# Opening stage of a two-block kernel: order of the loads, four more buffers for the modulation weights, and the memory norm summed on TensorE

## Chip, core and metric

The kernel runs on one core of a Trainium2 chip. A core has engines that each run their own list of instructions in order: TensorE (PE, with its weight loads as PEld), VectorE (DVE), ScalarE (ACT), GpSimd (POOL) and SyncE (SP). Data moves between HBM and on-chip memory by DMA; a DMA is issued by one of these engines, and in this kernel before the change by SP nearly always. The metric is the device time of one execution in microseconds (us), lower is better.

## The reference

The computation is two transformer blocks on 512 tokens of width 1024, in float32. The first block has two layers with a stream of 512 tokens and a context of 256 tokens; the second has latent attention, a long convolution (hyena), attention to 256 memory tokens, and a mixture of experts. The change touches what is needed at the start of the first block, and two things of the second block that depend on no activation and are made at the start:

```python
# first block, for l = 0 and 1
mx = jnp.split(silu_c @ w_mod[l] + b_mod[l], 6, axis=-1)      # "modulation", for the stream
mc = jnp.split(silu_cc @ w_mod[l] + b_mod[l], 6, axis=-1)     # and for the context
ax = modulate(rmsnorm(h, norm1_g[l]), mx[0], mx[1])
ac = modulate(rmsnorm(hc, norm1_g[l]), mc[0], mc[1])
yx, yc = mixing_layer(ax @ w_in[l], ac @ w_in[l], ...)         # pool mixing, neighborhood attention, retention
# second block
kf = _hyena_filters(S, hy_w1, hy_b1, hy_freq, hy_w2, hy_b2, hy_w3, hy_b3, hy_decay)
k, v = jnp.split(_rms(mem, mem_norm_g) @ w_mkv, 2, axis=-1)   # keys and values of the memory
```

`_hyena_filters` is two sine layers of width 64, a third layer times an exponential decay, and a Fourier transform over 512 positions (a product with a matrix here).

## The kernel before

Activations lie with channels on the partitions, 8 tiles of 128 channels by 512 tokens (256 for the context and the memory). A product with a weight keeps float32 accuracy by three matmuls on parts (L198 to L200): the weight is loaded (L180, 512 KB a piece, tile `wraw`, 4 buffers), rounded by ACT (L181, `whi`) and its remainder made by DVE (L182, `wlo`); the activation has a rounded part (L268 or L348, names ending in h) and a remainder (L269 or L349, names ending in l).

`first()` (L1671) makes the opening from generators, each of which does one step when it is asked: `memory()` (letter m), `modulation(0, 0)` (d), `hyena_filters()` (f), the loads of the stream (h) and the norm of the stream (n). The strings `START` and `SECOND` say whose turn it is. A tile scheduler then puts the instructions of all engines in an order, in which each engine runs its own, without overtaking. SP's list of DMA issues is one such order: an issue whose buffer is not free yet, or whose data are not there yet, holds up all issues behind it. Each of SP's DMAs also waits until the eighth before it has landed.

- `modulation(l, r)` makes a third of the six modulation vectors of a layer: 16 loads of 512 KB (L409, tile `mraw`, 2 buffers), each read by a pair of float32 matmuls with 2 columns of output partitions (L412, tile `bg`); at the end ACT copies the sums (L417, `mrow`), four small matmuls turn them (L420) and DVE adds the bias (L424). r = 0 holds what the first norm needs; r = 1 and 2 are taken a step at a time beside the neighborhood attention and the retention of layer 0 (`beside` and `tick`).
- `memory()` loads the 256 memory tokens (L1446), norms them, and makes keys (8 pieces of `w_mk`, written to HBM by L1456) and values (8 pieces of `w_mv`, written by L1472). Its norm is the common one: ACT squares a tile (L327), POOL adds it to a sum (L328, `sqacc`), PE sums over the partitions into a column (L301), ACT takes the square root (L289), DVE the reciprocal (L290), PE spreads it over the partitions again (L314), ACT copies it (L317, `rstd`), DVE multiplies (L340).
- `hyena_filters()` makes the two sine layers (L1147, and L1115 to L1125 for the sine; ACT's last step gives `hh`), the third layer (L1173, with L1175 the exponential and L1176 the product) and the transform, and writes it to HBM (`kf`, L1201; `kx`, L1210).
- After the opening, layer 0 begins: the norm of stream and context with the modulation (`ah`, `al`), the pool mixing (`pool_steps`: products with `w_in` into the `lin` and `sc` banks, which ACT copies to `px`, L825; POOL adds windows, L842 to L853), then for each pair of heads the neighborhood attention (`na_unit`: scores L240, softmax L498) and the retention (`ret_pair`). The bias of the neighborhood attention is loaded and masked by POOL (L580, L583) once the pool mixing's memory is free.

Of the kernel before, what the change touches and what calls it, by code (L numbers as in the profile page):

```python
# [11 lines left out]
F32 = mybir.dt.float32  # L12
# [3 lines left out]
ALU = mybir.AluOpType  # L16
AX = mybir.AxisListType

P = 128
# [33 lines left out]
START = "m f m m m f f f m m f m f m m h h h h h h d f h f d d d d h f d d f d f d d m m m f d m n f f f d d n m m d d n m m d d n m n".split()  # L53
# [52 lines left out]
class Builder:  # L106
    def __init__(self, ctx, tc, a, out):
        self.tc, self.nc, self.a, self.out = tc, tc.nc, a, out
        pool = lambda name, bufs=1, **kw: ctx.enter_context(tc.tile_pool(name=name, bufs=bufs, **kw))
        self.cp = pool("const")  # L110
        self.sm = None
        self.ps = pool("psum", 8, space=bass.MemoryType.PSUM)
        self.uid = 0
        self.background = iter(())
        self.opened, self.seconds = {}, {}
        self.np, self.nw, self.ahead = None, S, 2
        self.turn, self.probs, self.pinned = True, 2, False
        self.meanwhile = iter(())
# [283 lines left out]
    def modulation(self, l, r):  # L402
# [3 lines left out]
        for k in range(KC):  # L406
            for half in range(2):
                raw = self.t([P, 1024], F32, "mraw", 2, self.modp)
                nc.sync.dma_start(raw, self.a["w_mod"][l, r, k, half])  # L409
                for g in range(2):  # L410
                    q = 32 * (2 * half + g)
                    nc.tensor.matmul(ps[q:q + 2, :], self.csil[:, k, :], raw[:, g * 512:g * 512 + 512],  # L412
                                     start=k == 0, stop=k == KC - 1, tile_position=(0, q))
                yield
# [712 lines left out]
    def hyena_filters(self):  # L1127
# [32 lines left out]
        for n in range(2):  # L1160
# [49 lines left out]
            nc.sync.dma_start(self.kx[n].rearrange("o r s -> (o r) s"), o[:3, 0])  # L1210
# [230 lines left out]
    def memory(self):  # L1441
# [7 lines left out]
        self.norm(m, (0, C), lambda k: self.col("mem_norm_g_2", k), None, mh, ml)  # L1449
        yield  # L1450
        self.mk = self.tc.dram_tile([KC, P, C], F32, name="mk_dram")
        for j in range(KC):
            ps = self.linear(self.weight(a["w_mk"][j], 1024), mh, ml, (0, C))
            x = self.t([P, C], F32, "mo", 2)
            nc.scalar.copy(x, ps)
            nc.sync.dma_start(self.mk[j], x)  # L1456
            yield
# [10 lines left out]
        for j in range(2):  # L1468
# [3 lines left out]
            nc.sync.dma_start(self.mv[j], x)  # L1472
# [198 lines left out]
    def first(self):  # L1671
# [16 lines left out]

        memory = within(memory_pool, self.memory())
# [6 lines left out]
        self.close("memory")  # L1696
# [666 lines left out]
```

## Time and profile before

| | us |
|---|---|
| median of 3 runs | 2606.75 (2606.6 to 2607.93) |
| the profiled execution | 2606.64 |
| its span | 2604.8 |
| PE busy, whole span | 2461.1 (94%) |
| DVE, ACT, POOL busy | 1707.2, 1169.6, 434.0 |
| PE busy in the first 200 us | 171.17 |
| PE busy from 200 to 600 us | 383.93 of 400 |

Times in the trace count from the start of the span. The list of waits of an engine names the line that waited, what released it, the sum, the number and the longest. A timeline row has the start, the busy time, the engine and line, the operation with output and input tiles, a count, and in brackets the idle time before it with its releaser. A float32 matmul shows as two records, so that a pair of modulation matmuls is "x4". [...]

### The profile page before, as it was taken

What the parts mean: (1) busy time and instruction counts of PE and PEld (TensorE: products, weight loads), DVE (VectorE), ACT (ScalarE), POOL (GpSimd) and SP (SyncE); (2) the same over time, 40 slices, a digit from 0 to 9 for tenths busy, and PEclk for the clock granted to TensorE, in tenths of its full rate; (3) what the DMA queues carried; (4) which work ended last, traced back from release to release, by engine and by line L of the source; (5) the groups of instructions that cost most, each with busy time, mean ns of one, the idle gap of its engine ahead of it and who ended that gap; (6) DMA issues with size and microseconds to landing.
All of it is one profiled execution on the core that took longest, in us unless ns stands there. A gap on an engine that the chain in (4) does not pass through costs nothing. (4 is left out here: it accounts for less than half of the span.)

```text
span 2604.8 us, 37537 instructions
## 1 busy us (share of the span) xinstructions
PE 2461.1 (94%) x14286; PEld 2002.3 (77%) x14286; DVE 1707.2 (66%) x2916; ACT 1169.6 (45%) x1971; POOL 434.0 (17%) x448
## 2 busy tenths in 40 slices
PE   6999999999999999998999999999999879989996
PEld 5568766788888888887877888888878777866664
DVE  6656776657667666566777664545788987535555
ACT  6555456655322313355555553424665655421112
POOL 3042121120000000043232200000600352031100
PEclk9999999999999999999999999999999999989998
DMA  7742222252335353252111533332421453379992
GB/s 236 267 151 87 86 90 98 65 171 86 96 119 160 99 174 108 66 174 77 50 43 55 165 97 97 94 100 91 128 71 51 162 192 122 112 269 405 415 417 120
DMA packets 114047, 368.90 MB, mean 142 GB/s; under 512 B 17988, under 2 KB 29648, under 8 KB 101450
## 3 DMA queue, kind: packets, MB, share of 16 engines
q1 hardware_dynamic: 110554, 358.10, 40.8%
q0 software_dynamic: 3312, 8.40, 0.9%
q8 instruction: 113, 1.85, 0.3%
q14 instruction: 68, 0.56, 0.1%
HBM read 356.95 MB, written 13.68 MB: 142 GB/s over the span
## 5 line engine op out<-in xcount | busy, mean ns | idle before, releaser
L198 PE MATMUL lin<-ah,whi 128*128 128x512 f32 (+1 forms) x1504 | 556.3, 370 | 19.9 <-ACT qd L224 9.3
L200 PE MATMUL lin<-al,whi 128*128 128x512 f32 (+1 forms) x1504 | 547.6, 365 | 1.5 <-DVE al L349 1.1
L199 PE MATMUL lin<-ah,wlo 128*128 128x512 f32 (+1 forms) x1504 | 545.5, 363 | 2.8 <-DVE wlo L182 2.8
L181 ACT CAST whi<-wraw 128x1024 fp32r<-128x1024 f32 (+2 forms) x297 | 297.5, 1004 | 309.6 <-PE sc L200 171.0
L182 DVE TENSOR_TENSOR wlo<-wraw,whi 128x1024 fp32r<-128x1024 f32 (+2 forms) x297 | 360.7, 1216 | 83.3 <-ACT whi L181 82.1
L198 PEld LDWEIGHTS lin<-ah,whi 128*128 128x128 f32 x1504 | 286.7, 191 | 69.8 <-ACT qd L224 11.2
L200 PEld LDWEIGHTS lin<-al,whi 128*128 128x128 f32 x1504 | 285.8, 190 | 50.0 <-issue 2.7
L199 PEld LDWEIGHTS lin<-ah,wlo 128*128 128x128 f32 x1504 | 286.6, 191 | 40.6 <-DVE wlo L182 3.3
L328 POOL TENSOR_TENSOR sqacc<-sqacc,sq 128x256 f32<-128x256 f32 (+1 forms) x101 | 129.7, 1289 | 1083.6 <-ACT sq L327 1082.3
L199 PE MATMUL sc<-ah,wlo 128*128 128x256 f32 (+1 forms) x696 | 219.7, 316 | 0.0
L198 PE MATMUL sc<-ah,whi 128*128 128x256 f32 (+1 forms) x696 | 219.6, 316 | 0.0
L200 PE MATMUL sc<-al,whi 128*128 128x256 f32 (+1 forms) x696 | 219.0, 316 | 0.0
L198 PEld LDWEIGHTS sc<-ah,whi 128*128 128x128 f32 x696 | 132.8, 191 | 10.7 <-issue 0.9
L199 PEld LDWEIGHTS sc<-ah,wlo 128*128 128x128 f32 x696 | 133.0, 191 | 10.0 <-DVE wlo L182 0.4
L200 PEld LDWEIGHTS sc<-al,whi 128*128 128x128 f32 x696 | 132.7, 191 | 8.1
L892 DVE SCALAR_TENSOR_TENSOR fv<-lin,vec,fv 128x511 f32<-128x511 f32 x67 | 50.1, 749 | 117.1 <-ACT fv L891 117.1
L450 DVE CUSTOM_DVE_ANT_0 mraw<-mraw,crow 128x512 f32<-128x512 f32 x128 | 86.8, 689 | 42.5 <-DMA mraw<-in_w_mod_rows 41.3
L199 PE MATMUL lin<-mh,wlo 128*128 128x512 f32 (+1 forms) x292 | 105.3, 361 | 1.5 <-DVE wlo L182 1.4
L198 PE MATMUL lin<-mh,whi 128*128 128x512 f32 (+1 forms) x292 | 105.3, 361 | 0.0
L200 PE MATMUL lin<-ml,whi 128*128 128x512 f32 (+1 forms) x292 | 104.8, 359 | 0.0
L1924 PE MATMUL lin<-ew,ex 128*64 128x256 f32 x864 | 98.7, 381 | 0.3 <-issue 0.3
L891 ACT ACTIVATE fv<-lin,vec 128x512 f32<-128x512 f32 x67 | 52.1, 778 | 102.1 <-PE lin L200 85.6
(642 smaller groups left out, 5297.8 us busy)
## 6 DMA issues: line engine op xcount, KB each, us to landing
ew<-in_w_moe SPq DMA_DIRECT2D x81, 1024.0 KB, 16.6
wraw<-in_w_up SPq DMA_DIRECT2D x88, 512.0 KB, 3.5
wraw<-in_w_in SPq DMA_DIRECT2D x61, 512.0 KB, 3.7
mraw<-in_w_mod SPq DMA_DIRECT2D x48, 512.0 KB, 3.5
mraw<-in_w_mod_rows SPq DMA_DIRECT2D x96, 256.0 KB, 2.8
wraw<-in_w_down SPq DMA_DIRECT2D x48, 448.0 KB, 3.3
wraw<-in_w_out SPq DMA_DIRECT2D x32, 512.0 KB, 3.6
wraw<-in_w_down SPq DMA_DIRECT2D x16, 512.0 KB, 3.5
```

The source lines that it names most:

```text
L181: nc.scalar.copy(hi[:, :n], raw[:, :n])
L182: nc.vector.tensor_tensor(out=lo[:, :n], in0=raw[:, :n], in1=hi[:, :n], op=ALU.subtract)
L198: mm(out, wh, xh, start=start, stop=False)
L199: mm(out, wl, xh, start=False, stop=False)
L200: mm(out, wh, xl, start=False, stop=stop)
L328: nc.gpsimd.tensor_tensor(out=acc, in0=acc, in1=sq, op=ALU.add)
L450: self.tc.keep_in_program_order(nc.vector.tensor_tensor_reduce(out=x, in0=raw, in1=self.crow[:, i, d], scale=1.0, scalar=0.0, op0=ALU.mult ...
L891: nc.scalar.activation(out=v[:, t0:t1], in_=ps, func=AF.Identity, scale=cw(1), bias=self.col("conv_b", 44 * l + f))
L892: nc.vector.scalar_tensor_tensor(out=v[:, t0 + 1:t1], in0=ps[:, :t1 - t0 - 1], scalar=cw(0), in1=v[:, t0 + 1:t1], op0=ALU.mult, op1=ALU.add)
L1924: self.pin(nc.tensor.matmul(ps[CAP * f:CAP * f + CAP, :256], xk, pieces(512 * k + 256 * f, 256), start=k == 0, stop=k == KC - 1, tile_posi ...
```

## The change

The string `START` is replaced: the filters' first step comes first, and from then on the memory's and the modulation's steps take turns from the beginning. The loads of `modulation(0, 0)` take their tiles from a pool of their own with 4 buffers (`modq`), open until `START` is used up; the later ones use the old pool with 2. For r = 1 and 2 of each layer the first matmul of each pair is kept in program order by the scheduler. The memory's norm squares its 8 tiles on ACT and DVE in turn, and 8 float32 matmuls with a 128x128 matrix of ones sum them over the partitions, so that each partition has the sum; the root and the reciprocal are taken of the 128x256 tile. The writes of `kx`, of the memory's keys and of its values are issued by ACT.

```diff
-START = "m f m m m f f f m m f m f m m h h h h h h d f h f d d d d h f d d f d f d d m m m f d m n f f f d d n m m d d n m m d d n m n".split()
+START = "m f m d m d f m d f m d f m d f m d m d f d m d f m d h f m d h f m d h f m d h f d h m f d h d h m d h n f n m n m n m n f".split()
...
         for k in range(KC):
             for half in range(2):
-                raw = self.t([P, 1024], F32, "mraw", 2, self.modp)
-                nc.sync.dma_start(raw, self.a["w_mod"][l, r, k, half])
+                pool, engine = (self.modp, nc.sync) if self.modq is None else self.modq
+                raw = self.t([P, 1024], F32, "mraw", 2 if self.modq is None else 4, pool)
+                engine.dma_start(raw, self.a["w_mod"][l, r, k, half])
                 for g in range(2):
                     q = 32 * (2 * half + g)
-                    nc.tensor.matmul(ps[q:q + 2, :], self.csil[:, k, :], raw[:, g * 512:g * 512 + 512],
-                                     start=k == 0, stop=k == KC - 1, tile_position=(0, q))
+                    ins = nc.tensor.matmul(ps[q:q + 2, :], self.csil[:, k, :], raw[:, g * 512:g * 512 + 512],
+                                           start=k == 0, stop=k == KC - 1, tile_position=(0, q))
+                    if r > 0 and g == 0:
+
+                        self.tc.keep_in_program_order(ins)
...
-            nc.sync.dma_start(self.kx[n].rearrange("o r s -> (o r) s"), o[:3, 0])
+            nc.scalar.dma_start(self.kx[n].rearrange("o r s -> (o r) s"), o[:3, 0])
...
-        self.norm(m, (0, C), lambda k: self.col("mem_norm_g_2", k), None, mh, ml)
+
+        ps = self.psum("pt")[:, :C]
+        for k in range(KC):
+            sq = self.t([P, C], F32, "mo", 2)
+            if k % 2:
+                nc.vector.tensor_tensor(out=sq, in0=m[k], in1=m[k], op=ALU.mult)
+            else:
+                nc.scalar.activation(out=sq, in_=m[k], func=AF.Square)
+            nc.tensor.matmul(ps, self.ones, sq, start=k == 0, stop=k == KC - 1)
+        r = self.t([P, C], F32, "mr", 1)
+        nc.scalar.activation(out=r, in_=ps, func=AF.Sqrt, scale=1.0 / D, bias=self.eps)
+        nc.vector.reciprocal(out=r, in_=r)
+        for k in range(KC):
+            nc.vector.tensor_tensor(out=m[k], in0=m[k], in1=r, op=ALU.mult)
+            self.affine_split(mh[k], ml[k], m[k], self.col("mem_norm_g_2", k))
         yield
...
-            nc.sync.dma_start(self.mk[j], x)
+            nc.scalar.dma_start(self.mk[j], x)
...
-            nc.sync.dma_start(self.mv[j], x)
+            nc.scalar.dma_start(self.mv[j], x)
...
+        self.modq = self.open("modq", "right"), nc.sync
...
-        self.close("memory")
+        self.close("modq", "memory")
+        self.modq = None
```

Line numbers of the changed kernel are up to 22 higher than those of before: its L181 is L180 of before, L411 is L409, L414 is L412, L1152 is L1147, L1178 is L1173, L1475 is L1456, L1733 is L1711, L302 and L315 are L301 and L314, L830 is L825. L1459, L1461 and L1462 are the new squares and their products.

SP's list of DMA issues, between the first loads of `w_mk` and the first load of the modulation; before:

```order
L1711 DMA hy_87<-in_hT 128x768
L1711 DMA hy_88<-in_hT 128x768
L1456 DMA mk_dram<-mo_251 128x256
L180 DMA wraw_536<-in_w_mk 128x1024
L1456 DMA mk_dram<-mo_285 128x256
L180 DMA wraw_570<-in_w_mk 128x1024
L1456 DMA mk_dram<-mo_319 128x256
L1711 DMA hy_89<-in_hT 128x768
L1711 DMA hy_90<-in_hT 128x768
L1711 DMA hy_91<-in_hT 128x768
L1456 DMA mk_dram<-mo_429 128x256
L409 DMA mraw_611<-in_w_mod 128x1024
```

and after, from the first load of `w_mk` on:

```order
L181 DMA wraw_222<-in_w_mk 128x1024
L411 DMA mraw_257<-in_w_mod 128x1024
L181 DMA wraw_261<-in_w_mk 128x1024
L411 DMA mraw_295<-in_w_mod 128x1024
L1162 DMA hskip_300<-in_hy_skip 1x1024
L1168 DMA hw_304<-in_hy_w3b 65x1024
L1170 DMA hdec_306<-in_hy_decay 128x1024
L181 DMA wraw_344<-in_w_mk 128x1024
L411 DMA mraw_378<-in_w_mod 128x1024
L181 DMA wraw_400<-in_w_mk 128x1024
L411 DMA mraw_434<-in_w_mod 128x1024
L181 DMA wraw_456<-in_w_mk 128x1024
```

Before, a write of keys (`mk_dram`) stands ahead of nearly every further load, and the first `mraw` comes behind four of these writes; after, loads of `w_mk` and `mraw` take turns, with no write among them.

ACT's list where the modulation r = 0 is done and the norm of the stream begins; before, from the last copy of `mrow` on:

```order
L417 COPY mrow_72<-bg_610 2x512 x4
L193 CAST wlo_1180<-wraw_1179 128x1024
L289 ACT_TABLE_LOAD
L289 ACTIVATE tokw_1077<-pt_1072,eps 128x4
L1471 COPY mvo_1068<-sc_764 128x512
L1471 COPY mvo_1068<-sc_765 128x512
L1198 COPY hodd_1130<-lin_1116 128x512
L317 COPY rstd_1085<-pt_1080 128x512
L181 CAST whi_1262<-wraw_1261 128x1024
```

and after, from the last casts of filter n = 0 on (the copies of `mrow` stand some thirty rows further up):

```order
L269 CAST hs1h_849<-hx_912 128x512
L1180 ACTIVATE he_965<-hdec_837,htc_121 128x512
L1214 COPY ho_809<-pt_800 4x512
L1180 ACTIVATE he_970<-hdec_837,htc_121 128x512
L1215 DMA kx_dram<-ho_809 3x512
L290 ACT_TABLE_LOAD
L290 ACTIVATE tokw_1048<-pt_1043,eps 128x4
L269 CAST hs0h_842<-hx_973 128x512
L318 COPY rstd_1056<-pt_1051 128x512
L269 CAST hs1h_850<-hx_977 128x512
L1180 ACT_TABLE_LOAD
L1180 ACTIVATE he_1060<-hdec_837,htc_121 128x512
```

The root (L290) of the stream's norm now has a copy for the filters (`ho`) and the issue of its write (`kx_dram`) ahead of it, and the exponentials of the second filter (L1180) behind it, with a load of the function table on either side.

PE's list at the pool mixing's products with `w_in`; before, with the first two loads' pairs of r = 1:

```order
L199 MATMUL lin_1273<-ah_1094,wlo_1263 128x512
L200 MATMUL lin_1273<-al_1102,whi_1262 128x512
L301 MATMUL pt_1325<-cmat,sqacc_1302 128x1 x2
L412 MATMUL bg_1805<-mraw_1806,csil 2x512
L198 MATMUL lin_1273<-ah_1095,whi_1262 128x512
L199 MATMUL lin_1273<-ah_1095,wlo_1263 128x512
L412 MATMUL bg_1805<-mraw_1806,csil 2x512
L412 MATMUL bg_1805<-mraw_1930,csil 2x512 x2
L198 MATMUL sc_1336<-ah_1091,whi_1268 128x512
```

and after, where the first of these pairs stands now, in the neighborhood attention:

```order
L199 MATMUL lin_1759<-ah_1085,whi_1754 128x512
L200 MATMUL lin_1759<-ah_1085,wlo_1755 128x512
L201 MATMUL lin_1759<-al_1093,whi_1754 128x512
L278 MATMUL pt_1785<-cmat,pr_1748 128x128 x4
L414 MATMUL bg_1795<-mraw_1796,csil 2x512 x2
L278 MATMUL pt_1816<-cmat,vw_1812 128x128 x2
L241 MATMUL sc_1821<-k_1589,qd_1565 128x256
```

Five loads' pairs of r = 1 stood between rows 455 and 594 of PE's list, among the pool mixing's products, two of them split; now they stand at rows 719, 785, 848, 1010 and 1034, each whole. From row 2401 of 11966 on, PE's list is the same in both.

## Rows read from the trace of the kernel before

**Rows 1.** Waits of PE before 215 us: line, releaser, us, times, longest.

```profile
PE pt L301 <- POOL sqacc L328: 14.1, 1, 14.1
PE bg L412 <- DMA mraw<-in_w_mod: 4.7, 2, 3.6
PE pt L1173 <- ACT hh L1125: 3.7, 1, 3.7
```

**Rows 2.** Windows of 25 us from 0 to 200, their sum.

```profile
sum 200.00, PE 171.17 PEld 117.47 DVE 118.03 ACT 111.59 POOL 57.36; mean PE 21.40 PEld 14.68 DVE 14.75 ACT 13.95 POOL 7.17
```

**Rows 3.** Waits of SP's queue, 0 to 125 us.

```profile
SPq L1456 <- ACT mo L1455: 31.6, 7, 8.9
SPq L409 <- PE bg L412: 29.4, 13, 5.5
```

**Rows 4.** Windows: at half clock, the fullest of DMA, the modulation's stretch.

```profile
44.90:55.30 10.40, 10.40 (x26) 6.30 (x27) 5.54 (x7) 6.42 (x10) 2.55 (x2) 0.51 0.48 179
120.00:130.00 10.00, 10.00 (x52) 7.44 (x50) 2.54 (x7) 7.29 (x11) 0.00 (x0) 1.00 0.95 365
61.60:128.30 66.70, 64.71 (x249) 34.19 (x249) 41.83 (x55) 35.53 (x55) 5.41 (x5) 1.00 0.76 264
```

**Rows 5.** Timeline of ACT, POOL and DVE from modulation to softmax.

```profile
128.97 1.28 ACT L289 ACT_TABLE_LOAD   x1
...
158.60 0.57 ACT L825 COPY px<-lin 128x512 f32<-128x512 f32 x1
...
169.75 0.66 POOL L842 TENSOR_TENSOR pxx<-px 128x287 f32<-128x287 f32 x1 [3.49 <-ACT px L825]
...
189.94 2.21 POOL L211 MEMSET ql<- 64x512 f32 x4
...
201.71 0.69 DVE L498 CUSTOM_DVE_ANT_0 pr<-sc,bias 128x512 f32<-128x512 f32 x1 [6.12 <-PE sc L241]
```

**Rows 6.** Timeline of PE: after the sine, the modulation's end, a pair that waits.

```profile
44.88 3.55 PE L1173 MATMUL pt<-hw,hh 65*128 65x512 f32 x4 [3.73 <-ACT hh L1125]
...
124.46 1.03 PE L412 MATMUL bg<-mraw,csil 128*2 128x512 f32 x4
...
128.32 0.95 PE L420 MATMUL pt<-cmat,mrow 128*128 128x8 f32 x8
...
181.37 1.60 PE L412 MATMUL bg<-mraw,csil 128*2 128x512 f32 x4 [3.63 <-DMA mraw<-in_w_mod]
```

**Rows 7.** Timeline of the memory's norm: SP's first filter load, POOL, PE.

```profile
1.65 0.90 SPq L1446 DMA_DIRECT2D mm<-in_mT  x2
2.59 0.58 SPq L1136 DMA_DIRECT2D hyv<-in_hyv  x1
...
8.53 5.53 POOL L328 TENSOR_TENSOR sqacc<-sqacc,sq 128x256 f32<-128x256 f32 x7 [6.24 <-ACT sq L327]
...
20.57 0.58 PE L198 MATMUL lin<-mmh,whi 128*128 128x256 f32 x1 [1.77 <-ACT mmh L348]
```

**Rows 8.** DMA issues, 0 to 135 us: count, KB, us to landing.

```profile
mraw<-in_w_mod SPq DMA_DIRECT2D x17, 512.0 KB, 3.5
...
kf_dram<-ho SPq DMA_DIRECT2D x5, 512.0 KB, 5.8
...
mm<-in_mT SPq DMA_DIRECT2D x2, 512.0 KB, 6.8
```

**Rows 9.** Reciprocals and a product on DVE: count, busy us, mean ns.

```profile
L508 DVE RECIPROCAL smx<-smx 128x1 f32<-128x1 f32 x17 | 2.7, 160 | 7.7 <-ACT pr L506 7.7
...
L290 DVE RECIPROCAL tokw<-tokw 128x4 f32<-128x4 f32 x1 | 0.2, 179 | 0.8 <-ACT tokw L289 0.8
...
L340 DVE TENSOR_TENSOR nx<-mm,rstd 128x256 f32<-128x256 f32 x8 | 3.0, 407 | 0.0
```

**Rows 10.** PE from 200 to 600 us: windows' sum, and what L412 waited for.

```profile
sum 400.00, PE 383.93 PEld 306.18 DVE 268.28 ACT 225.87 POOL 81.23; mean PE 47.99 PEld 38.27 DVE 33.53 ACT 28.23 POOL 10.15
...
  DMA mraw<-in_w_mod: 2.2, 4
```

More of the change, by code (lines that the diff above doesn't have):

```diff
@@ L50 @@
 CONV = "a a a * b a b * * a a a b * a b a * b c c b b b * c b c * d d c c * c d * c d c d d d d d + +".split()
-START = "m f m m m f f f m m f m f m m h h h h h h d f h f d d d d h f d d f d f d d m m m f d m n f f f d d n m m d d n m m d d n m n".split()
+START = "f m f m d m d f m d f m d f m d f m d m d f d m d f m d h f m d h f m d h f m d h f d h m f d h d h m d h n f n m n m n m n f".split()
 SECOND = "f n n n n f f n f n n f n".split()
@@ L1695, in first @@
             next(steps[t], None)
-        self.close("memory")
+        self.close("modq", "memory")
+        self.modq = None
         self.big = self.open("acts")
```

## Prediction

> **What bounds the kernel now.** TensorE bounds the kernel: its idle time before the first softmax, and the time it runs at half clock, are all that the opening can give. The list of PE's waits [rows 1] names the three that matter there: 14.1 us at the very start for POOL's sum of squares, 3.7 for the sine's result `hh`, 4.7 for two loads of the modulation. The windows [rows 2] give the total: PE is busy 171.17 of the first 200 us, so 28.8 are idle, half of them before it has begun. The queue of SP says why loads are late [rows 3]: it stood 31.6 us at the writes of the memory's keys until ACT had made the data, with all later loads behind them, and 29.4 us for one of the two `mraw` buffers. The DMA engines are not what holds the loads: over the modulation's stretch they moved 264 GB/s at a share of 0.76, in ten microseconds of it 365 at 0.95 [rows 4]. [...]
>
> What ends the opening is a chain through other engines [rows 5, 6]: the modulation's small matmuls at 128.32 on PE, the norm, the copies to `px` at 158.60, POOL's mixing until 189.94, the bias's loads and masks, the first softmax at 201.71. So the question is how much earlier the modulation is done, and what of that this chain lets through.
>
> **The change part by part.**
>
> *The memory's norm.* Out go seven adds on POOL (5.53 us), the column sums and the spreading. Five small filter loads now go ahead of the tokens' loads; at 0.58 each these come 2.9 us later, at about 4.6 [rows 7]. From issue to landing they took 6.8, a load of 512 KB in a quieter queue 3.5 [rows 8], so the tokens are there between 8 and 11.4; I take 10.5. Eight products of 256 columns follow on PE. None is in the trace; the nearest row has two float32 matmuls of 512 columns in 3.55 us at half clock [rows 6], so one of 256 costs 0.89 at half clock, 0.44 at full. PE has just started, and I take 0.89: 7.1 in all, until about 18. The root and the multiplication follow as before, and a reciprocal over 256 elements, which no row shows. Bounds: 0.41, as the product of that shape, and, from 160 ns for one element and 179 for four [rows 9], 6.3 ns an element, 1.8 us. I take 1.8, since the slope is that of the operation itself. The memory's first matmul comes at about 21, where it was at 20.57 [rows 7]: nothing gained there, the products hidden in time in which PE waited. If the tokens come at 8, 2.5 us are gained; if at 11.4 with a slower reciprocal, 1 to 2 lost.
>
> [...] The rows above, up to four elements, can't show whether 256 cost more. [...]
>
> *Filters first.* The first sine matmul no longer waits for the norm, and the second stands ahead of the memory's matmuls, so `hh` is there some 10 us earlier and the wait of 3.73 goes. If the idle time goes, the clock has nothing to fall after: the 10.40 us at 0.51 are 5.3 at full clock, 5.1 gained [rows 4]. What is late next is the weights of the memory's keys, paced by the loads.
>
> *Loads of the modulation.* The writes leave SP's queue and four buffers stand where two did. Counted from SP's new list, 27.3 MB go until the last `w_mv` piece; at 365 GB/s that is 75 us, at 264 it is 103 [rows 4], and some forty matmuls at about 0.24, ten us, stand behind it on PE: 113 at the slow end, so the loads don't set the modulation's end before PE's own work does. PE's list until there: four of the third layer's matmuls and nine of the transform's fewer (0.89 each at full clock, and 0.24, since twelve of them stand between the end of the pair of 124.46 and 128.32: 5.7 us, done later instead), the eight products more (7.1). With PE's start 4 us earlier, the 3.7 and 5.1 above, and 1 to 5 us of waits for loads and small stalls: 128.3 - 4 - 5.7 + 7.1 - 3.7 - 5.1 - 3 is 113.9, and between 108 and 118. I take 113. Of the lone pairs that other work splits, 5 of 16 where 2 were, I put 0.5 us in that sum's bounds.
>
> *From the modulation to the softmax.* Before, the copies to `px` began 30.3 us after the modulation's matmuls [rows 5, 6]. Now three things lie in the norm's way on ACT: the copy `ho` ahead of the root waits until a filter's write has left its buffer (two adds on DVE and a landing of 5.8 [rows 8], about 10 us from the modulation's end, with some 5 us of work for PE meanwhile): 5 us; two more function tables at 1.28 [rows 5]: 2.6; and the copies to `px` stand behind the context's norm. So `px` at 113 + 30.3 + 7.6, about 151, and 148 to 156. Behind it POOL's mixing took 31.3, in which POOL waited 3.49 for the context's `px` [rows 5]; these now come together with the others, so 27.8: until 179. Then 11.8 to the softmax as before, which makes 191, and 187 to 197: **10.7 us earlier**. PE would be ready sooner: it loses some 18 us less idle time and 5 at half clock, and has five pairs less, so at about 178. POOL sets the end, not PE.
>
> *The pairs of r = 1.* Five pairs leave the pool mixing, at 1.03 a pair 5.1 us, and with them the wait of 3.63 for a load [rows 6], which is in the 18 above. They go into the neighborhood attention, where from 200 to 600 us PE idles 16.1 of 400 [rows 10]: hidden at best, 5.1 us at worst, 2.5 taken. The pinned pairs with two buffers meet a reload that lands after 3.5 with about as much other work between: 0 to 1 us in each of four places in the retention, 2 taken; pairs no longer split give 2 back.
>
> *Writes on ACT.* Twelve issues of about a third of a microsecond on an engine that is busy 111.6 of 200 us [rows 2]: hidden, at most 4 us if the norm stands behind them, which only the one priced above does.
>
> The sum: -10.7 + 2.5 + 2 - 2 = -8.2 against the profiled execution's 2606.64, which stands 0.1 under the median: **2598.4 us**.
>
> **The rivals.** (a) *PE sets the end.* If `px` comes at 146 or the mixing runs alone and faster, the softmax comes as soon as PE is ready, 178 to 184: 18 to 22 us earlier, less the 2 to 5 that go into the attention: 2589. For it: PE's idle time is 28.8 [rows 2]. Against: POOL's 27.8 don't shrink with the loads. (b) *The norm gives it back.* The filter's write ahead of the root, the tables and the context's norm cost 15 rather than 7.6, or the modulation ends at 118: softmax at 197 to 198, 4 us, eaten by the pairs: 2604.5. For it: these waits are in line on ACT, where a wait stops everything. (c) *The loads come no sooner.* If SP is still held up early, moves 179 GB/s for 20 us, as from 44.9 to 55.3 [rows 4], and 264 after that, the last `w_mv` piece lands at 110; some forty matmuls of PE's list at 0.24 stand behind it, the modulation ends at 120, and the softmax is 4 us earlier, less the pairs: 2605. [...] (d) *Slower.* Kept in program order, a pair whose load is not there stops PE, where before other matmuls went ahead; SP's queue stands ahead of that load for other buffers. One such wait cost 3.63 [rows 6]; before, such waits sum to only 2.2 from 200 to 600 [rows 10]. There are 27 pinned pairs left of 32; from 0.3 us each on, 8 us, the gain is gone, and at 0.5, 14 us: 2612.
>
> **How the numbers follow.** My forecast, 2594 to 2601, has 0.43; (a) 0.18; (b) 0.15; (c) 0.10; (d) 0.14. A measurement of this kernel tells some 0.2% from no change, 5.2 us: faster is below 2601.5. The forecast and (a) make faster 0.61; (b), (c) and the mildest of (d) make 0.27; slower 0.12. The range leaves out the far end of (a) and most of (d): 2586 to 2609.
>
> **What would show it.** In the profile after: memory's first matmul at 20 to 23; no wait of `hh`; a clock of 1.0 from 25 us on; SP without waits at the key writes; the modulation's small matmuls at 107 to 118; `px` at 148 to 156, the first softmax at 187 to 197, with POOL or the bias's loads as what it waits for; some 2 to 5 us more PE work from 200 to 540. I am wrong if the modulation ends past 120, if the softmax comes before 185 or after 199, or if L414's waits for loads from 200 us on exceed 8 us.

## The result and the profile after

The changed kernel takes 2625.17 us (median of four runs, 2623.78 to 2629.71) where the kernel before takes 2606.78: the ratio is 1.0074, with a 95% interval of 1.0062 to 1.0085. It is slower by 18.4 us. The profiled execution, 2629.71 us with a span of 2627.9, is the longest of the four, so that its trace holds some four to five microseconds more than the median. It is 23.1 us longer than that of the kernel before (2627.9 less 2604.8); the places below account for 19.4 of them.

PE's windows of the changed kernel, three of 25 us and the sum of the first 200 (columns: start and end, length, busy time and instructions of PE, PEld, DVE, ACT, POOL, then the granted clock of TensorE as a share of full speed, DMA share, GB/s):

```profile
0.00:25.00 25.00, 15.05 (x48) 7.58 (x48) 14.80 (x33) 11.49 (x21) 1.72 (x7) 0.94 0.84 309
...
100.00:125.00 25.00, 19.06 (x68) 13.71 (x66) 8.50 (x11) 13.54 (x25) 7.83 (x8) 0.86 0.73 248
125.00:150.00 25.00, 21.64 (x66) 13.21 (x67) 18.59 (x34) 17.36 (x28) 0.00 (x0) 0.73 0.14 50
...
sum 200.00, PE 170.48 PEld 114.92 DVE 110.12 ACT 112.82 POOL 45.26; mean PE 21.31 PEld 14.36 DVE 13.77 ACT 14.10 POOL 5.66
```

The start is better: DMA moves 309 GB/s in the first 25 us, where it moved 272. But PE is busy 170.48 of 200 us, as before [rows 2]: its idle time is not less, it stands elsewhere, and from 100 to 150 us the granted clock was 0.86 and 0.73 besides, where it was 1.00 and 0.93. The list of PE's waits before 215 us shows where it stands now:

```profile
PE lin L199 <- ACT qd L225: 5.7, 1, 5.7
PE pt L1152 <- DMA hw<-in_hy_w: 5.1, 1, 5.1
PE pt L278 <- POOL vw L591: 4.1, 1, 4.1
PE sc L199 <- ACT mvo L1490: 3.5, 1, 3.5
PE lin L199 <- ACT mmh L349: 3.0, 2, 2.7
```

The three waits of [rows 1] are gone: the 14.1 us for POOL's sum, the 3.7 for `hh`, the 4.7 for loads. Apart from the 5.1 us at the very start, until the filters' weights are there, what ends the idle time now is mostly ACT and POOL. The same stages as in [rows 5, 6, 7], from PE's timeline of the changed kernel:

```profile
8.62 5.41 PE L1462 MATMUL pt<-mo,cmat 128*128 128x256 f32 x14 [1.55 <-ACT mo L1461]
...
20.60 0.39 PE L199 MATMUL lin<-mmh,whi 128*128 128x256 f32 x1 [2.74 <-ACT mmh L349]
...
93.90 1.04 PE L414 MATMUL bg<-mraw,csil 128*2 128x512 f32 x8
...
118.39 0.79 PE L199 MATMUL sc<-hs1h,whi 128*128 128x512 f32 x1 [3.49 <-ACT mvo L1490]
...
123.67 1.22 PE L425 MATMUL pt<-cmat,mrow 128*128 128x8 f32 x8
...
132.30 1.70 PE L302 MATMUL pt<-cmat,sqacc 128*128 128x1 f32 x8
```

and from ACT's, POOL's and DVE's:

```profile
97.26 1.17 ACT L422 COPY mrow<-bg 2x512 f32<-2x512 f32 x2
...
117.75 1.07 ACT L1490 COPY mvo<-sc 128x512 f32<-128x512 f32 x2 [3.79 <-DMA mv_dram<-mvo]
...
172.74 0.56 ACT L830 COPY px<-lin 128x512 f32<-128x512 f32 x1
...
173.45 1.09 POOL L847 TENSOR_TENSOR pxx<-px 128x543 f32<-128x543 f32 x1 [1.54 <-ACT px L830]
...
199.72 2.21 POOL L212 MEMSET ql<- 64x512 f32 x4
...
208.21 0.69 DVE L503 CUSTOM_DVE_ANT_0 pr<-sc,bias 128x512 f32<-128x512 f32 x1 [6.12 <-DMA bias<-in_rpb]
```

The last pairs of the modulation run at 93.90, some 30 us before those of [rows 6], and ACT's last copy of the sums (`mrow`) begins at 97.26. But the small matmuls L425 run only at 123.67, since PE's list has them behind matmuls that wait for ACT; the column sums of the norm come 8.6 us after them, where before they came 0.8 after (129.13); the copies to `px` come at 172.74 instead of 158.60. From there POOL's mixing takes 27.0 us instead of 31.3, and the first softmax is 6.5 us late.

That is a third of the loss. The rest comes behind the first softmax. Windows of the kernel before between the first softmax of each of the three pairs of heads, and up to the retention's first norm sums:

```profile
201.70:251.20 49.50, 47.70 (x358) 41.78 (x358) 36.43 (x82) 27.09 (x60) 10.18 (x18) 1.00 0.29 92
251.20:297.20 46.00, 45.91 (x351) 38.95 (x350) 32.12 (x75) 24.01 (x54) 7.32 (x12) 1.00 0.26 75
297.20:382.20 85.00, 76.43 (x486) 56.48 (x484) 65.43 (x128) 43.57 (x94) 18.28 (x24) 1.00 0.32 103
```

and of the changed kernel between the same points:

```profile
208.20:266.10 57.90, 53.26 (x373) 42.91 (x373) 37.23 (x82) 27.62 (x60) 10.11 (x18) 0.97 0.29 81
266.10:312.90 46.80, 46.39 (x351) 39.04 (x350) 32.50 (x75) 23.47 (x54) 7.41 (x12) 1.00 0.33 96
312.90:401.60 88.70, 77.79 (x487) 59.03 (x486) 64.99 (x129) 42.02 (x91) 18.66 (x24) 0.98 0.24 81
```

The stretch takes 193.4 us instead of 180.5: 8.4 more in the first pair of heads, where PE has 5.6 us more work and 2.8 more idle time, 0.8 in the second, 3.7 in the third. With the 6.5 of the opening that is 19.4. A part of the 8.4 comes from the opening too: POOL's mixing ended 9.8 us late (199.72 instead of 189.94), of which the softmax shows 6.5, and PE then waits 4.1 us for POOL's `vw` (the list above), where it waited 0.9. Behind this wait the granted clock was 0.50 from 213.0 to 216.4 us, which is why the row has 0.97.

### The profile page after: what moved, and what is told of

Its sections match the earlier page's. It is cut to its first block, busy times and chain, and to the rows that moved or that the text cites. A ratio compares the mean times of both kernels' runs of the same rounds, so it can differ in the third digit from the quotient of the medians.

```text
span 2627.9 us, 37530 instructions
## 1 busy us (share of the span) xinstructions
PE 2476.7 (94%) x14294; PEld 2011.6 (77%) x14294; DVE 1701.1 (65%) x2920; ACT 1172.5 (45%) x1969; POOL 424.5 (16%) x441
## 5 line engine op out<-in xcount | busy, mean ns | idle before, releaser
L329 POOL TENSOR_TENSOR sqacc<-sqacc,sq 128x256 f32<-128x256 f32 (+1 forms) x94 | 122.0, 1303 | 1131.5 <-ACT sq L328 1130.8
L201 PEld LDWEIGHTS sc<-al,whi 128*128 128x128 f32 x696 | 132.3, 191 | 8.3 <-DVE al L270 0.3
```

Source lines behind the costliest of these rows:

```text
L201: mm(out, wh, xl, start=False, stop=stop)
L329: nc.gpsimd.tensor_tensor(out=acc, in0=acc, in1=sq, op=ALU.add)
```

## The experiments

All runs are compared with the kernel before on the same chip, where that took 2605.5 to 2608.5 us. The table has the ratio with its interval, and from each profiled execution when the modulation's small matmuls, the norm's column sums, the first copy to `px` and the first softmax began, and how long it took from there to the retention's first norm sums. The places come from one execution each, which can lie some microseconds off the median, so that they and the ratio need not agree: f5 is 9.6 us later than the kernel before at the retention's sums and 2 us slower in the end, a_oldstart 5.3 later and 10 slower.

| kernel | ratio | modulation | sums | px | softmax | to retention |
|---|---|---|---|---|---|---|
| before | 1 | 128.3 | 129.1 | 158.6 | 201.7 | 180.5 |
| after | 1.0074 [1.0062, 1.0085] | 123.7 | 132.3 | 172.7 | 208.2 | 193.4 |
| a_oldstart | 1.0040 [1.0026, 1.0054] | 122.9 | 123.8 | 152.0 | 197.0 | 190.5 |
| a_nopin | 1.0013 [1.0003, 1.0022] | 121.1 | 128.9 | 169.3 | 206.2 | 180.0 |
| a_spwrites | 1.0068 [1.0051, 1.0085] | 115.5 | 129.3 | 169.5 | 204.9 | 193.2 |
| b_newstart | 1.0048 [1.0031, 1.0065] | 122.8 | 134.2 | 176.1 | 213.7 | 179.5 |
| b_pin | 1.0034 [1.0020, 1.0049] | 128.3 | 129.1 | 157.9 | 201.2 | 186.7 |
| b_newnorm | 1.0035 [1.0018, 1.0051] | 131.6 | 132.4 | 165.0 | 209.3 | 180.7 |
| c1_noorder_nopin | 1.0014 [1.0003, 1.0025] | 122.1 | 123.0 | 155.1 | 203.4 | 177.7 |
| c4_norm_first | 1.0047 [1.0030, 1.0063] | 122.3 | 124.5 | 183.7 | 218.0 | 183.1 |
| d7_px_first | 1.0085 [1.0068, 1.0101] | 122.7 | 131.3 | 168.2 | 213.2 | 191.8 |
| d10_before_px_first | 1.0021 [1.0012, 1.0031] | 127.4 | 128.2 | 154.6 | 202.1 | 184.9 |
| d12_values_halves | 1.0046 [1.0029, 1.0063] | 116.5 | 127.7 | 167.1 | 202.5 | 191.5 |
| d13_all_three | 1.0018 [1.0008, 1.0027] | 114.6 | 127.5 | 166.5 | 216.2 | 171.6 |
| f1_nopin_halves | 1.0015 [1.0005, 1.0025] | 115.5 | 130.6 | 173.2 | 209.8 | 180.6 |
| f2_nopin_halves_oldstart | 0.9994 [0.9984, 1.0004] | 123.7 | 124.6 | 161.0 | 201.7 | 175.2 |
| f3_before_four_buffers | 0.9991 [0.9981, 1.0000] | 124.4 | 125.2 | 157.2 | 200.0 | 180.0 |
| f4_buffers_actwrites | 0.9999 [0.9990, 1.0008] | 124.3 | 125.3 | 163.2 | 203.2 | 178.1 |
| f5_nopin_halves_oldnorm | 1.0009 [0.9999, 1.0018] | 114.7 | 128.4 | 175.0 | 211.7 | 180.2 |
| c7_buffers_newnorm | 1.0005 [0.9996, 1.0014] | 126.7 | 127.6 | 158.4 | 198.3 | 184.9 |

### Which part: order, pins, or writes

Three causes stood against each other: the new order of the opening (O), the pairs kept in program order (P), the writes on ACT (W).

```diff
 a_oldstart: the changed kernel, START as before
-START = "f m f m d m d f m d f m d ...
+START = "m f m m m f f f m m f m f ...
 a_nopin: the changed kernel without
-                    if r > 0 and g == 0:
-                        self.tc.keep_in_program_order(ins)
 a_spwrites: the changed kernel, for kx, mk and mv
-            nc.scalar.dma_start(self.mk[j], x)
+            nc.sync.dma_start(self.mk[j], x)
 b_newstart: the kernel before, START as after
```

> The changed kernel with the old START string; all else of the change stays (four buffers, pinned pairs, memory norm by products, writes on ACT). Theory O (the new order puts the second filter's steps and the context's norm among the stream's norm, so that the copies to px came at 172.7 us where they came at 158.6): px back at 150 to 160, first softmax at 195 to 203, time 2605 to 2614. Theory P (the pairs of r = 1 kept in program order, five of which moved into the neighborhood attention, cost the time): no change, 2622 to 2628. Theory W (the writes on ACT): no change, 2622 to 2628.

> The changed kernel without the rule that keeps the pairs of r = 1 and 2 in program order. Theory P: the 8.4 us lost between the first and the ninth softmax of the neighborhood attention come back, 2615 to 2618. Theory O: the pairs only move back into the opening, first softmax later by 2 to 5 us and the attention shorter by as much, 2621 to 2628. Theory W: no change.

> The changed kernel with the writes of kx, keys and values issued by SP again. Theory W (ACT stood 3.8 us for a write of values to land, and its later copies with it): the copies to px and the first softmax 4 to 8 us earlier, 2616 to 2621. Theory O: SP's queue stands at the writes again, the modulation's loads end later than 95 us, the time is 2622 to 2632.

> The kernel before with the new START string alone. Theory O: px after 165, first softmax after 206, time 2613 to 2625. Theories P and W: near the kernel before, 2600 to 2609.

Measured: 2617.4, 2611.3, 2625.9 and 2619.4 us. The writes on ACT are out as a cause: with the writes on SP the time is the same. Of the two others neither was alone: without the pins 14 of the 18 us are gone, more than theory P gave them, with the old order 8, which is less than theory O asked for, although `px` and the softmax came where it had them (152.0 and 197.0). The new order alone costs the kernel before 0.48%, with `px` and the softmax as late as theory O said.

What the order does in the opening shows best in a_spwrites, where ACT copies the values without that wait (115.43) and PE has none for the copies:

```profile
115.52 1.06 PE L425 MATMUL pt<-cmat,mrow 128*128 128x8 f32 x8 [0.61 <-DVE he L1181]
...
129.31 1.71 PE L302 MATMUL pt<-cmat,sqacc 128*128 128x1 f32 x8
```

The modulation's small matmuls are 8 us earlier than in the changed kernel, the norm's column sums only 3. Five runs have the modulation at 114.6 to 116.5 and the sums at 127.5 to 130.6. POOL has made what the sums need by 111.0 us in the changed kernel, and between its matmuls L425 and the sums PE's list has only products of the filters. So with the new order it is the place behind these, and not the modulation, that sets when the norm begins. From the sums to `px` the table has 39 to 47 us in the runs with the new order and 28 to 38 in those with the old (leaving out the four that move the filter's or the context's steps themselves); what makes this second difference isn't shown.

How the pins cost time is seen by counting. A pair shows as four records (two matmuls of two records each). The group of PE's modulation matmuls (count, busy us, mean ns, idle before), in the first line up to the first softmax, in the second from there to the retention's sums, of the changed kernel:

```profile
L414 PE MATMUL bg<-mraw,csil 128*2 128x512 f32 x64 | 17.3, 605 | 0.0
L414 PE MATMUL bg<-mraw,csil 128*2 128x512 f32 x60 | 14.4, 592 | 0.4 <-DMA mraw<-in_w_mod 0.4
```

and the same two of a_nopin:

```profile
L414 PE MATMUL bg<-mraw,csil 128*2 128x512 f32 x120 | 31.0, 606 | 5.1 <-DMA mraw<-in_w_mod 5.0
L414 PE MATMUL bg<-mraw,csil 128*2 128x512 f32 x16 | 4.1, 592 | 0.0
```

Without the pins 30 pairs run ahead of the first softmax, with them 16. These 14 pairs are 13.7 us of PE's time (31.0 less 17.3) and PE stood 5.0 us more for loads, and yet the softmax came 2.1 us **earlier**: pairs in the opening cost nothing that shows, since PE waits there for other engines in any case. Behind the softmax the pinned kernel has 11 pairs more, 10.3 us, and its stretch is 13.4 us longer: there each pair costs at least its full price. The windows of a_nopin behind the softmax, where the pairs no longer are:

```profile
206.20:261.70 55.50, 49.62 (x357) 43.48 (x356) 35.51 (x82) 26.92 (x60) 10.00 (x18) 0.94 0.26 85
261.70:305.30 43.60, 43.00 (x338) 38.76 (x338) 31.26 (x76) 23.07 (x54) 7.42 (x12) 1.00 0.21 55
305.30:386.20 80.90, 72.64 (x469) 57.13 (x468) 64.67 (x129) 44.24 (x95) 18.55 (x24) 1.00 0.19 63
```

The first of these windows is only 2.4 us shorter than that of the changed kernel, although no pair stands in it: PE waits 4.9 us for POOL's `vw` here as well, and the clock is 0.94. So that delay isn't the pins'.

### The pins alone, and what is left without pins and order

From this came theory F: pairs are free in the opening and cost their full price afterwards.

```diff
 b_pin: the kernel before with
+                    if r > 0 and g == 0:
+                        self.tc.keep_in_program_order(ins)
 c1_noorder_nopin: the changed kernel, START as before, no pins
 b_newnorm: the kernel before with the memory's norm by products
```

> The kernel before with the pairs of r = 1 and 2 kept in program order, nothing else. Theory F (in the opening PE idles at waits of other engines, and pairs taken there are free; in the attention and retention PE is the bound and each pair costs its full 0.96 us, and a pinned pair no longer fills a wait): opening up to the first softmax no more than 3 us shorter than 201.7, from there to the retention's first sums of rd 189 to 192 us where before took 180.5, time 2612 to 2617. Rival (the pins cost only beside the new loads with four buffers): 2604 to 2609.

> The changed kernel with the old START and without the pins: what is left of the change is the four buffers, the memory's norm by products and the writes on ACT. If the two causes add up (START +10, pins +12 of the 18 lost), the softmax comes at 195 to 201 and the stretch after it takes 178 to 182: 2598 to 2604. If the four buffers, norm or writes cost something by themselves: 2606 to 2612.

> The kernel before with the memory's norm by products alone. PE begins at about 9 instead of 14.1; if the memory's matmuls are earlier by 2 to 4 us and the half clock after hh stays, 2602 to 2606; if the loads pace the rest, 2606 to 2609.

b_pin gave 2616.7, +0.34%, as theory F forecast. The softmax is 0.5 us earlier for five pairs less, and the stretch behind it 6.2 us longer, which is less than the 8.5 to 11.5 that the theory gave it:

```profile
201.20:253.90 52.70, 51.43 (x373) 41.62 (x372) 36.29 (x83) 27.50 (x60) 10.35 (x18) 1.00 0.32 96
253.90:300.70 46.80, 46.34 (x350) 38.99 (x350) 32.56 (x74) 23.51 (x54) 7.28 (x12) 1.00 0.35 96
300.70:387.90 87.20, 77.70 (x487) 59.27 (x487) 64.99 (x129) 42.10 (x91) 18.65 (x24) 0.98 0.26 82
```

In the first window PE has 3.7 us more work and no more idle time, which is four pairs. In the last one it has 8 pairs where the kernel before has 10, and yet takes 2.2 us longer. The same wait of PE for ACT's `rx` shows why; in the kernel before,

```profile
339.48 1.03 PE L412 MATMUL bg<-mraw,csil 128*2 128x512 f32 x6
342.15 0.39 PE L198 MATMUL lin<-ah,whi 128*128 128x256 f32 x1 [1.64 <-ACT rx L694]
```

and in b_pin, with the window behind it:

```profile
345.63 0.39 PE L198 MATMUL lin<-ah,whi 128*128 128x256 f32 x1 [2.68 <-ACT rx L696]
346.90:350.40 3.50, 3.50 (x18) 3.40 (x17) 2.63 (x4) 2.13 (x4) 3.11 (x3) 0.51 0.00 0
```

Unpinned, a pair and a half ran in the wait. Pinned, none does, the wait is 1.0 us longer, and the granted clock falls to 0.51 behind it, where it was 1.00 from 342.10 to 346.90 in the kernel before.

c1, 2612.1, shows that the causes don't add: beside it a_nopin has the new order and the same ratio (1.0014 and 1.0013), while with the pins the order costs 0.34%. Nor is the order free wherever the pins are missing: it costs 0.48% alone, and 0.21% between f2 and f1 below. The pins cost time in all four pairs of runs that differ by them alone: 0.61% (a_nopin and the changed kernel), 0.34% (b_pin), 0.26% (c1 and a_oldstart) and 0.31% (f1 and d12).

b_newnorm missed both expectations. The norm by products alone makes the kernel before 0.35% slower, with PE beginning at 8.5 us instead of 14.1 and the memory's first matmul no earlier. This cost isn't the norm's own: f5 and f1 below differ by the norm alone and are alike, f4 and f2 too, and c7 has it at 1.0005. What follows came later (the modulation at 131.6, `px` at 165.0), and in the first 50 us the granted clock was 0.86 instead of 0.95; which change of the lists did it is not shown.

### Inside the opening: what is between the column sums and the softmax

```diff
 c4_norm_first: a_nopin, and the last two filter steps moved from START to SECOND
-START = "... m d h n f n m n m n m n f"
-SECOND = "f n n n n f f n f n n f n"
+START = "... m d h n n m n m n m n m"
+SECOND = "n n n f n f f f n f f n f n n f n"
 d7_px_first: the changed kernel; ACT's first step of the norm, with
 self.hold set in layer 0 while the context's norm is made
+            if self.hold:
+                self.tc.keep_in_program_order(ins)
 d10_before_px_first: the same on the kernel before
 d12_values_halves: the changed kernel
-            x = self.t([P, D], F32, "mvo", 1)
             for i in range(2):
-                nc.scalar.copy(x[:, 512 * i:512 * i + 512], acc[2 * j + i])
-            nc.scalar.dma_start(self.mv[j], x)
+                x = self.t([P, 512], F32, "mvo", 2)
+                nc.scalar.copy(x, acc[2 * j + i])
+                nc.scalar.dma_start(self.mv[j][:, 512 * i:512 * i + 512], x)
 d13_all_three: a_nopin with d7 and d12
```

> The changed kernel without the pins, and with the last two filter steps of START moved into SECOND, behind three steps of the norm. Theory O (second filter's work stands between the norm's column sums and px): px at 150 to 160 and the first softmax at 193 to 200, time 2598 to 2605. Rival (the context's norm ahead of the copies to px does it, which stays): px after 165, time 2609 to 2613, as without the pins alone.

> The changed kernel with the context's norm kept in program order on ACT, so that the copies of the stream's px stand ahead of the context's norm (ACT row 158 instead of 173); all else as in the change. Theory A (the place of px behind the context's norm delays POOL's mixing): px at 166 to 168 instead of 172.7, first softmax 3 to 6 us earlier than 208.2, time 2619 to 2622. Rival B (the mixing then waits for the context's px, as with the old START, or DVE and POOL slow each other): softmax within 2 us of 208.2, time 2623 to 2627.

> The changed kernel with the memory's values copied and written in halves of 512 columns with two buffers of that size, so that ACT's copy doesn't wait for the first write to land (3.8 us) and PE not for ACT's copy (3.5 and 1.4 us). Theory V (this wait delays the second filter and the norm behind it): the norm's column sums 3 to 6 us before 132.3, first softmax 3 to 6 us earlier, time 2619 to 2622. Rival: the second filter waits for something else, within 2 us, 2623 to 2627.

> The changed kernel without the pins, with px ahead of the context's norm and the values in halves. If each is worth what its own run shows and they add: 2611 less 3 to 8, 2603 to 2608. If they share one slack: 2608 to 2612.

> The kernel before with the context's norm kept in program order on ACT, so that px comes ahead of its last two casts (ACT rows 147 and 148 instead of 155 and 156), nothing else. Theory A: first softmax 1 to 3 us earlier, 2604 to 2607; rival B: 2606 to 2610.

c4 (2620.9) missed the times of both expectations: the sums come 2.2 us after the modulation, as hoped, but `px` at 183.7, since the copies still stand behind the whole norm of the context, which itself is later. So I took the copies out from behind it, d7, and theory A fell too: `px` 4.6 us earlier, the softmax 5.0 us **later**, 2629.9. POOL's timeline of d7 shows why:

```profile
169.65 1.09 POOL L850 TENSOR_TENSOR pxx<-px 128x543 f32<-128x543 f32 x1
...
183.74 0.66 POOL L850 TENSOR_TENSOR pxx<-px 128x287 f32<-128x287 f32 x1 [7.54 <-ACT px L833]
```

POOL begins 3.8 us earlier and then stands 7.54 us for the context's `px`, which waits for the norm that now runs beside POOL's own work. The mixing ends when both streams are there; which one comes first is a trade. On the kernel before the same edit, d10, costs 0.21%: the softmax is where it was (202.1, although `px` was at 154.6), and the stretch behind it 4.4 us longer, for which no cause is shown. d12 gave 6.9 us (2618.3), a little more than theory V forecast, but it doesn't show V: ACT still stood for writes of values, in two places now:

```profile
114.39 0.58 ACT L1490 COPY mvo<-sc 128x512 f32<-128x512 f32 x1 [0.50 <-DMA mv_dram<-mvo]
...
119.51 0.58 ACT L1490 COPY mvo<-sc 128x512 f32<-128x512 f32 x1 [3.07 <-DMA mv_dram<-mvo]
```

What changed is that the modulation's small matmuls ran at 116.5, ahead of the matmul that waits for this copy, and that the clock was 0.97 from 100 to 125 us instead of 0.86. d13 brought 2609.8, no better than the pins' removal alone.

### What adds, and what the useful parts are worth

```diff
 f1_nopin_halves: the changed kernel, no pins, values in halves
 f2_nopin_halves_oldstart: f1, START as before
 f5_nopin_halves_oldnorm: f1, memory's norm as before
 f3_before_four_buffers: the kernel before; in START's modulation
+                pool = self.modp if self.modq is None else self.modq
+                raw = self.t([P, 1024], F32, "mraw", 2 if self.modq is None else 4, pool)
 f4_buffers_actwrites: f2, memory's norm as before
 c7_buffers_newnorm: the kernel before with four buffers and the norm by products
```

> The changed kernel without the pins and with the values in halves; the new START and the norm by products stay. If the two causes add (2625.2 less 13.9 for the pins, less 6.9 for the wait): 2602 to 2606, the softmax at 199 to 202. If they share one slack: 2609 to 2612, the softmax near 206.

> As the run before, and with the old START: four buffers, norm by products, writes on ACT with the values in halves. If all three add: 2596 to 2601. If they share one slack, or the copies to px, which stand behind most of the context's norm here too (ACT row 169), cost what the order saves: 2605 to 2612.

> The kernel before with four buffers of the modulation in the opening, nothing else. If the four buffers alone bring the modulation forward: small matmuls at 120 to 126 instead of 128.3, time 2600 to 2605. If the queue behind the key writes decides: 127 to 129, 2605 to 2609.

> As the run f1 (no pins, halves, new START), with the memory's norm as before (squares summed on POOL). If the norm by products costs by itself (as alone on the kernel before, +8.6): 3 to 9 us faster than f1. If it hides: within 3 us of f1.

> The kernel before with four buffers and the writes on ACT, values in halves; old START, old norm, no pins. If the parts left over give a gain of their own, 2600 to 2604 beside 2607 to 2608 of before; if only places in the order move, 2604 to 2612.

> The kernel before with four buffers and the norm by products; old START, writes on SP, no pins. The norm alone cost 8.6 on the kernel before, at the memory's start PE was ready no earlier: if that cost is the norm's own, 2611 to 2617; if it came from where the scheduler put the rest, 2603 to 2610.

f1 (2611.7) is like a_nopin (2611.3): the gains of the halves and of the missing pins don't add. With pins the halves were worth 6.9 us, without them nothing. f2, f3, f4 and c7 lie between 0.9991 and 1.0005 of the kernel before. So no run here has a part of the change that gives a gain clear of the noise; f3, the four buffers alone, and f2, all without order and pins, are the best, and neither is shown to be faster. f3 does bring the modulation 4 us forward (124.4, as expected) and the softmax 1.7, and no more comes through: 2607.1 us, not the 2600 to 2605 that this was to give.

## Why the prediction was wrong, point by point

Two terms of the sum failed. The opening stood in it with -10.7 us and came out at +6.5 in the trace; the pairs of r = 1 stood with +2.5, and the stretch that they went into came out 12.9 us longer, in part by the late opening. The step that failed in the first is the one from the loads to the softmax: it took the sum of PE's work for the modulation's end, and the modulation's end, with 7.6 us of waits on ACT, for the start of the norm and of `px`. In the second it is the price: a pair taken out of PE's waits was counted as half hidden where it went.

- **What bounds the kernel.** The first sentence of the reading failed: that PE's idle time in the opening is all that can be gained there. The idle time is not PE's to give back. The three waits of [rows 1] were removed as forecast and PE's busy time in 200 us remained 170.5 of 200; the idle time went to waits for ACT and POOL.
- **The memory's norm** came out close to what was worked out, its end in part by luck: eight products from 8.62 to 14.94, 6.3 us (7.1 taken), the reciprocal 1.74 (1.8 taken), the memory's first matmul at 20.60 (about 21 forecast). The tokens landed at 8.15, at the early end of 8 to 11.4, and the 2.5 us that this was to give didn't come: ACT's table load (1.28 us, to 16.49), a sine step on DVE ahead of the reciprocal and one behind it stood between, and the two errors made up for each other. The reciprocal's row in the changed kernel:

```profile
L1465 DVE RECIPROCAL mr<-mr 128x256 f32<-128x256 f32 x1 | 1.7, 1735 | 0.0
L1467 DVE TENSOR_TENSOR mm<-mm,mr 128x256 f32<-128x256 f32 x8 | 2.9, 411 | 0.0
```

  It is 4.2 times the product of that shape (1735 ns beside 411), so the measurement decides for the rows' slope, the upper of the two bounds. The slower reciprocal in the forecast's "1 to 2 lost" is shown by no run.
- **Filters first.** The wait for `hh` went, as forecast. The 5.1 us in the sum took the half clock [rows 4] for a consequence of that wait [rows 6], which was my estimate. That the clock then has nothing to fall after was wrong: it was 0.93 from 25 to 50 us, and from 100 to 150 us, among the idle times of the new waits, two windows had 0.86 and 0.73.
- **Loads of the modulation.** The loads were right, the step from them to the modulation's end was not. The last pairs ran at 93.90, within the 75 to 103 us that the forecast gave the loads, and the small matmuls at 123.67, outside 108 to 118. I took PE's work for the bound and summed it. In the list these matmuls stand behind others that wait for ACT's copies of the values (3.5 and 1.4 us) and a cast (2.4), from 100 us on at a lower clock (0.86 from 100 to 125 us), and a sum of work doesn't see that. And where the waits for the copies of the values were missing (a_spwrites, 115.52) the modulation ended inside the range and nothing was gained, since the sums stood behind the filters' products.
- **Writes on ACT** were priced as hidden, at most 4 us. The wait that I named behind them (the filter's write ahead of the root) didn't matter; one that I hadn't named did stand there: the second copy of values has one buffer with the first and waited 3.79 us for its write to land. What the writes' move is worth as a whole is nothing that can be measured: with the writes on SP the time was 2625.9. I had read the 31.6 us of [rows 3] as the reason why the loads are late, and that reading failed. In a_spwrites SP stands at the keys' writes again, 28.0 us, and yet the last pairs of the modulation run no later than in the changed kernel (93.90):

```profile
SPq L1475 <- ACT mo L1474: 28.0, 8, 13.2
92.29 1.04 PE L414 MATMUL bg<-mraw,csil 128*2 128x512 f32 x8
```

  With the writes gone SP's queue stood for other things, the weights' buffers and `mraw` (waits of SP's queue of the changed kernel, 0 to 125 us: line, releaser, us, times, longest):

```profile
SPq L193 <- DVE wlo L183: 18.9, 5, 6.5
SPq L411 <- PE bg L414: 18.4, 7, 4.6
SPq L181 <- DVE wlo L183: 12.4, 5, 9.4
SPq L1206 <- DVE ho L1205: 11.1, 3, 6.0
```

- **From the modulation to the softmax.** 37.9 us forecast to `px`, 49.1 measured. The terms that I had (filter's write, tables, context's norm, 7.6 in all) were the right kind, but the second filter's work, now inside the norm, wasn't priced, neither on ACT nor on PE, where the sums alone came 8.6 us behind the modulation instead of 0.8. POOL's part was forecast well: 27.8, measured 27.0; then 8.5 instead of 11.8. Which of the order's terms costs how much isn't told apart: c4 and d7 each moved one, and both lost time. That part of the cause stays open.
- **The pairs of r = 1** are the other term that was mis-sized. I counted their removal into PE's readiness, which by the prediction itself doesn't set the end of the opening, and took half of their price afterwards, 2.5 us. The runs showed: no gain in the opening (0.5 us for five pairs, b_pin; minus 2.1 for fourteen, a_nopin), and behind it 6.2 us in b_pin, 13.4 between a_nopin and the changed kernel. I had said that the 16.1 us of idle time from 200 to 600 us could hide them. Pinned, a pair goes where the program has it, not where PE waits; it leaves the waits longer, and after one of them, 2.68 us in b_pin, the granted clock was 0.51.
- **The rivals.** (d) was on the right side with the wrong mechanism: pinned pairs do make the kernel slower, but not by waits for their loads (L414 waited 0.4 us for loads from 215 to 600 us); they no longer stand in PE's waits. (b), the norm gives it back, was right in kind and too mild: it had 15 us more between modulation and `px` than before, and 18.8 came (49.1 less 30.3), but not through the first of its three waits, the filter's write. (c) was wrong in its first step, since the loads did come sooner. (a) could not come true as long as PE waits for what POOL and ACT make.

## To carry to other kernels

Before idle time of the bounding engine is counted as a gain, ask what it waits for, and what the scheduler puts into it: here work that filled a wait was free, and cost at least its full time where PE was busy, so an instruction kept in program order should be priced as if it stood in the busiest place. A scheduled kernel answers even a small edit with another order; the norm by products cost 0.35% alone and nothing that can be measured beside other edits, so run each part alone, and in more than one surrounding, before they are joined.

## What the runs showed of the hardware

A reciprocal of 256 elements on each partition took 1.735 us, close to the 1.8 worked out from the slope of two small ones (160 ns for one element, 179 for four).

The eight float32 products of 256 columns at the start of the kernel took 6.3 us, 0.79 each. That lies near the 0.89 worked out from half clock. Of their sixteen records the six that began before 11.3 us took 634 to 796 ns, the nine from 11.6 us on 379 to 483. The trace's first record of the granted clock is at 11.6 us, with 1.00 until 21.8, so the clock isn't shown to be the reason for the longer ones; that PE starts at half clock was an estimate.

After PE had waited 2.68 us in b_pin the granted clock was 0.51 for 3.5 us; at the same place of the kernel before, after a wait of 1.64 us, it stayed at 1.00.
